# Three edits to a float32 hybrid decoder layer: single PSUM banks in the first feed-forward layer, weight sums made in place, three load buffers

## The chip, the core and the metric

The kernel runs on one core of a Trainium2 chip. Times are device microseconds of that core. The time before is 1018.22 us, the median of three runs (1017.96 to 1020.32). One more execution was profiled. It took 1021.12 us, and the span from its first to its last instruction is 1019.4 us.

Five engines work side by side, each through its own queue in order: TensorE (PE, its weight loads PEld), VectorE (DVE), ScalarE (ACT), GpSimd (POOL) and SyncE (SP), whose queue issues most DMAs. They wait for each other by semaphores.

## The reference

One decoder layer over 512 tokens and 16 learned meta tokens (528 rows), width 1024, all in float32: a half-step SwiGLU feed-forward layer, a mixer with a gated short convolution group and a forgetting-attention group, a second half-step feed-forward layer, and a last norm.

```
h = h + 0.5 * swiglu_ffn(rms_norm(h, ffn1_norm), ffn1_w_gu, ffn1_w_down)
h = h + hybrid_mixer(rms_norm(h, mix_norm), w_in, conv_w, b_f, ...) 
h = h + 0.5 * swiglu_ffn(rms_norm(h, ffn2_norm), ffn2_w_gu, ffn2_w_down)

def swiglu_ffn(h, w_gu, w_down):
    gate, up = jnp.split(h @ w_gu, 2, axis=-1)
    return (jax.nn.silu(gate) * up) @ w_down
```

`w_gu` is 1024 x 5632 and `w_down` 2816 x 1024. The change is in the two feed-forward layers.

## The kernel before

**Split operands.** Activations lie transposed (128 of the 1024 columns by tokens). Every operand is split into a high and a low part of a faster matmul type, and each product is three matmuls: high by high, high by low, low by high. ScalarE makes the high part (`hi`, line 497, a CAST into `w_hi`), VectorE the low part (`lo`, line 501, into `w_lo`). The DMA-loaded weight tile is `raw`.

**Seven products for eight.** Most of a feed-forward layer runs in *units*. A unit multiplies a 2 x 2 block of weight tiles M11, M12, M21, M22 (for `nj` pairs of row blocks) by two halves of the tokens, with seven products in place of eight, by sums of weights and sums of activations. `prep` (line 460) loads and makes the weights, `products` (line 513) writes the matmuls. A gate or an up unit has `nj` = 4, here called wide; a `down` unit has `nj` = 3, 2 or 4. A product is 3 `nj` matmuls, so a unit of `nj` = 4 has 84.

**Weight sums before.** Two tiles are loaded for a unit: `raw["all"]` (all four blocks, line 474) and `raw["ss"]` (M11 and M12 a second time, line 470). Two DMAs from POOL's queue add to `ss` in flight (`add`, line 478), M12 and M22, so that it holds M11+M12 and M12+M22. VectorE makes `s24` in a tile of its own (lines 482, 485): M12+M22+M11, and that plus M21. `hi` and `lo` are made of four sources: `nat` (M11 and M21), `ss`, `s24` and `22` (M22).

**Slots.** The order of the work is written out by `Slots`: a list of PE slots, one product each, and for every slot a list of tasks of the other engines, sorted by a priority, emitted behind the slot's matmuls. A unit that begins at slot b has seven slots:

- b: A = first product; b+1: the previous unit's last product (`p4`, into the previous B); b+2: second product into A; b+3: B (`s24`); b+4: E; b+5: B again; b+6: C; its own `p4` follows at b+8.
- ScalarE seeds B with -A (line 540, task at b+1, before slot b+3; bank A is read while slot b+2 waits to write it) and C with -B (line 541, task at b+4, before slot b+5).
- VectorE and ScalarE read A, B, C and E out between b+3 and b+9 (in `down`, line 609 and lines 612, 613 add them to `hT`).

A, B and C come in pairs used by turns, E is one bank. In the second feed-forward layer each is a tile of one bank from the pool `banks`. In the first, A, B and C are tiles `acc` of two banks each, one for each turn (`new1`, lines 624 and 735), so both turns of B, for example, are one tile.

**Around it.** `pair_forms` (line 371) makes the activation sums: four POOL operations (lines 379 to 382), then ScalarE and VectorE splits (lines 368, 369), as tasks `t1 + e` and one later. The first four hidden tiles of the first layer and the next ones (`classical`, line 407) are ordinary products. `Weights` feeds the mixer and has the first two hidden tiles; the fourth accumulator of that stage, `a3`, stays in PSUM and is multiplied there (lines 715, 746 to 749).

Of the kernel before, what the change touches and what calls it, by code (L numbers as in the profile page):

```python
# [14 lines left out]
P = 128  # L15
# [18 lines left out]
class Weights:  # L34
# [129 lines left out]
def layer(ctx, tc, x, meta, n1, gu1, dn1, nm, w_in, conv_w, b_f, g_conv, g_attn, w_out, n2, gu2, dn2, nf, out):  # L164
# [174 lines left out]
    class Ffn:  # L339
# [116 lines left out]
        def raw(self):  # L456
            return self.pool.tile([P, 2048], F32, name="raw", bufs=2).rearrange("p (k c) -> p k c", c=256)


        def prep(self, b, mat, c0, j0, nj):  # L460
# [26 lines left out]
            def src(nm_):  # L487
                if nm_ == "nat":
                    return raw["all"][:, :, 0]
                if nm_ == "22":  # L490
                    return raw["all"][:, 1::2, 1]
                return raw[nm_].rearrange("p a b c -> p (a b) c")
# [20 lines left out]
        def products(self, nj, rhs, w):  # L513
# [109 lines left out]
    with tc.tile_pool(name="ps1", bufs=3, space=PSUM) as ps1, tc.tile_pool(name="ps1s", bufs=2, space=PSUM) as ps1s:  # L623
# [5 lines left out]
        with tc.tile_pool(name="xin", bufs=1) as xin:  # L629
# [50 lines left out]
            with tc.manual_schedule(engines={mybir.EngineType.PE, mybir.EngineType.Activation, mybir.EngineType.DVE}):  # L680
# [34 lines left out]
                a3, tile_a = new1()  # L715
# [5 lines left out]
                row_rstd(sa)  # L721
            gp = ps1s.tile([P, 512], F32, name="sm")
# [7 lines left out]
        with tc.tile_pool(name="ffn1", bufs=1, reuse_waits="tile") as pool, tc.manual_schedule(engines=ENGINES):  # L730
            sl = Slots()
            (accB, tile_b), (accC, tile_c) = new1(), new1()
            bank_e = ps1s.tile([P, 512], F32, name="sm")
            ring = lambda j: 0 if j == 10 else RING + (j + 3) % 4 * 14 * 264
            F = Ffn(gu1, dn1, 264, GN1, pool, sl, [[t[:, 0], t[:, 1]] for t in (tile_a, tile_b, tile_c)] + [bank_e], 0, ring)
            W.raw_pool = pool


            def early(f, g, u):
                def gate():  # L740
                    stt(g, g, -0.5, rs, ALU.mult, ALU.mult)
# [525 lines left out]
```

## Time and profile before

| | us |
|---|---|
| median of three runs | 1018.22 |
| lowest, highest | 1017.96, 1020.32 |
| profiled execution | 1021.12 |
| its span | 1019.4 |
| mean granted PE clock | 0.987 of full |
| busy: PE, PEld | 955.9, 907.4 |
| busy: DVE, ACT, POOL | 771.8, 563.0, 350.6 |

By stretch of the span: start and first tiles to 38; classical tiles of the first layer to 93; its units to 405; mixer to 645; classical tiles of the second layer to 692; its units to 990; last norm to 1019.4. In the first layer's units (312 us) PE is busy 286.0 us, in the second's (298 us) 288.3 us, in the mixer (240 us) 238.4 us.

How to read it: PE's busy time is modelled from the starts of matmuls that overlap. A wait is clearer on PEld, the loading of weights before a matmul, as idle time with its releaser in brackets: `[0.68 <-ACT acc L540]` means that the engine stood idle for 0.68 us, until the ScalarE instruction of line 540 on tile `acc` was done.

### The profile page before, as it was taken

The numbers are of one execution on the slowest core, as the hardware profiler recorded it, in microseconds if no ns is written. First come the engines' busy times: TensorE is split into PE (matmuls) and PEld (weight loads), VectorE is DVE, ScalarE is ACT, GpSimd is POOL, SyncE is SP. The second block draws the span as 40 slices with busy tenths as digits, with TensorE's granted clock in tenths as the row PEclk, the third lists the DMA queues.
The fourth block names the chain that finished last, engine by engine and source line by source line (L and its number), as shares of the span: only waits on it lengthen the run. The fifth ranks groups of instructions, "written<-read, shape, count | busy, mean of one in ns | idle before, by whom it ended". The sixth has DMA issues, their size and how long they took to land.

```text
span 1019.4 us, 18073 instructions
## 1 busy us (share of the span) xinstructions
PE 955.9 (94%) x7022; PEld 907.4 (89%) x7022; DVE 771.8 (76%) x1252; ACT 563.0 (55%) x981; POOL 350.6 (34%) x323
## 2 busy tenths in 40 slices
PE   8899999999999987999999999999999999999995
PEld 8798999999999877989999978778998998999994
DVE  6688886787677877777767567788885887788755
ACT  5545545554556444675747555455644554566344
POOL 3356534433544462310000000265533553454302
PEclk9999999999999998999999999999998999999997
DMA  6327789869985674423322122258789979998932
GB/s 202 91 83 173 153 208 224 172 143 224 222 182 132 156 167 106 122 64 84 83 64 76 55 84 62 64 124 208 159 198 210 208 166 215 209 221 194 225 64 84
DMA packets 205414, 149.87 MB, mean 147 GB/s; under 512 B 6836, under 2 KB 204768, under 8 KB 205328
## 3 DMA queue, kind: packets, MB, share of 16 engines
q1 hardware_dynamic: 146176, 119.26, 38.6%
q0 software_dynamic: 59008, 28.93, 23.3%
q8 instruction: 55, 0.90, 0.4%
q10 hardware_dynamic: 144, 0.52, 0.1%
q14 instruction: 31, 0.25, 0.1%
HBM read 146.53 MB, written 2.10 MB: 146 GB/s over the span
## 4 chain that ended last, share of the span: by engine, by line
PE 47%; DVE 8%; issue 4%; ACT 3%; DMA 2%; POOL 1%; ACTq 0%; POOLq 0%; DVEq 0%
PE bank L527 21%; PE bank L318 17%; PE acc L527 3%; PE bank L1059 2%; DVE w_lo L501 2%; DMA ss<-in_ffn_w_down_dram 1%; DMA ss<-in_ffn_w_gu_dram 1%; PE bank L996 1%; PE bank L1026 1%; DVE arena L369 1%; ACT w_hi L497 1%; DVE w_lo L454 1%; PE sm L527 1%; PE bank L1226 1%; DVE xn L398 0%
## 5 line engine op out<-in xcount | busy, mean ns | idle before, releaser
L527 PE MATMUL bank<-arena,w_hi 128*128 128x256 f32 x1568 | 290.2, 287 | 11.8 <-ACT bank L540 5.0
L527 PE MATMUL acc<-arena,w_hi 128*128 128x264 f32 x1296 | 245.9, 289 | 26.1 <-ACT acc L540 17.6
L527 PEld LDWEIGHTS bank<-arena,w_hi 128*128 128x128 f32 x1568 | 248.2, 195 | 14.9 <-ACT bank L540 6.7
L527 PEld LDWEIGHTS acc<-arena,w_hi 128*128 128x128 f32 x1296 | 201.7, 190 | 34.5 <-ACT acc L540 24.4
L527 PE MATMUL bank<-arena,w_lo 128*128 128x256 f32 x784 | 224.1, 286 | 0.0
L318 PE MATMUL bank<-arena,w_hi 128*128 128x512 f32 (+2 forms) x896 | 203.3, 331 | 0.0
L527 PE MATMUL acc<-arena,w_lo 128*128 128x264 f32 x648 | 185.1, 286 | 0.0
L318 PEld LDWEIGHTS bank<-arena,w_hi 128*128 128x128 f32 x896 | 142.1, 188 | 15.5 <-DVE arena L973 0.2
L527 PEld LDWEIGHTS bank<-arena,w_lo 128*128 128x128 f32 x784 | 152.7, 195 | 0.0
L478 POOL DMA_DIRECT2D ss<-in_ffn_w_gu_dram x68 | 89.1, 1572 | 162.7 <-DVE w_lo L501 35.2
L501 DVE TENSOR_TENSOR w_lo<-raw,w_hi 128x1024 fp32r<-128x1024 f32 (+2 forms) x124 | 115.7, 952 | 28.3 <-ACT w_hi L497 27.7
L318 PE MATMUL bank<-arena,w_lo 128*128 128x512 f32 (+2 forms) x448 | 127.5, 331 | 3.9 <-DVE w_lo L454 3.9
L527 PEld LDWEIGHTS acc<-arena,w_lo 128*128 128x128 f32 x648 | 122.7, 189 | 0.3 <-DVE w_lo L501 0.2
L497 ACT CAST w_hi<-raw 128x1024 fp32r<-128x1024 f32 (+2 forms) x124 | 93.4, 758 | 31.3 <-PE bank L527 15.9
L478 POOL DMA_DIRECT2D ss<-in_ffn_w_down_dram x56 | 72.5, 1541 | 107.1 <-DVE w_lo L501 52.9
L497 ACT CAST w_hi<-ss 128x1024 fp32r<-128x1024 f32 (+2 forms) x62 | 59.1, 954 | 77.7 <-PE acc L527 32.5
L318 PEld LDWEIGHTS bank<-arena,w_lo 128*128 128x128 f32 x448 | 75.6, 188 | 13.6 <-DVE w_lo L454 6.0
L497 ACT CAST w_hi<-s 128x1024 fp32r<-128x1024 f32 (+2 forms) x62 | 59.2, 955 | 40.3 <-DVE s L485 34.6
L501 DVE TENSOR_TENSOR w_lo<-s,w_hi 128x1024 fp32r<-128x1024 f32 (+2 forms) x62 | 79.6, 1284 | 0.0
L81 DVE TENSOR_TENSOR w_lo<-raw,w_hi 128x1024 fp32r<-128x1024 f32 (+2 forms) x53 | 56.5, 1076 | 20.5 <-ACT w_hi L80 20.2
L501 DVE TENSOR_TENSOR w_lo<-ss,w_hi 128x1024 fp32r<-128x1024 f32 (+2 forms) x62 | 68.4, 1103 | 0.0
L80 ACT CAST w_hi<-raw 128x1024 fp32r<-128x1024 f32 (+3 forms) x54 | 44.0, 828 | 43.6 <-PE bank L318 35.4
(251 smaller groups left out, 1525.6 us busy)
## 6 DMA issues: line engine op xcount, KB each, us to landing
raw<-in_ffn_w_gu_dram SPq DMA_DIRECT2D x34, 1024.0 KB, 6.0
ss<-in_ffn_w_gu_dram SPq DMA_DIRECT2D x34, 512.0 KB, 4.9
ss<-in_ffn_w_gu_dram POOLq DMA_DIRECT2D x68, 256.0 KB, 6.1
raw<-in_ffn_w_down_dram SPq DMA_DIRECT2D x20, 768.0 KB, 4.7
raw<-in_w_in_dram SPq DMA_DIRECT2D x24, 512.0 KB, 4.1
raw<-in_ffn_w_gu_dram SPq DMA_DIRECT2D x16, 512.0 KB, 3.9
ss<-in_ffn_w_down_dram SPq DMA_DIRECT2D x20, 384.0 KB, 3.3
ss<-in_ffn_w_down_dram POOLq DMA_DIRECT2D x40, 192.0 KB, 5.7
```

The lines of the kernel that those rows point to most:

```text
L80: nc.scalar.copy(h, src)
L81: nc.vector.tensor_sub(lw, src, h.bitcast(F32))
L318: nc.tensor.matmul(ap, lhsT=wt[:, kw, :], rhs=mt[:, k, c0 - off:c1 - off], start=(first and a == 0 and b == 0), stop=(last and a == len(ks ...
L369: self.sl.at(t + 1, lambda: nc.vector.tensor_sub(lo, src(), hi.bitcast(F32)), 2)
L454: self.sl.at(t - 1, lambda: nc.vector.tensor_sub(w["w"][1], w["r"], w["w"][0].bitcast(F32)), 3)
L478: nc.gpsimd.dma_start(out=raw["ss"][:, :, i], in_=mat_j[:, i, :, c0 + P:c0 + 2 * P], accum_op=ALU.add)
L497: nc.scalar.copy(w[nm_][0][:, :m], src(nm_))
L501: nc.vector.tensor_sub(w[nm_][1][:, :m], src(nm_), w[nm_][0][:, :m].bitcast(F32))
L527: nc.tensor.matmul(bank, lhsT=wt[:, idx(j), :], rhs=r[:, form, part], start=(start and i == 0), stop=(i == last), skip_group_check=True)
L996: nc.tensor.matmul(t[:, o:o + c1 - c0], lhsT=qt[:, i * P:(i + 1) * P], rhs=kt[:, c0:c1], start=(b == 0), stop=(b == 1))
L1026: nc.tensor.transpose(o, sm[:, SOFF[i] + j * P:SOFF[i] + (j + 1) * P], ident)
L1059: nc.tensor.matmul(oo, lhsT=lt, rhs=rt, start=(a == 0 and n_ == 0), stop=(a == 1 and n_ == len(ops) - 1))
```

## The change

1. The first feed-forward layer moves out of the two-bank accumulator pool into the pool `banks`: A, B and C are now two tiles of one bank each, as in the second layer. `a3` is copied to SBUF by ScalarE first, like the other three.
2. `load_ss` and its tile go. `load` is a task at b-15 rather than b-10. ScalarE copies M11 (`base`, at b-11) into a small tile `s3`; POOL's two adding DMAs (still at b-10) put M22 onto M12 inside the loaded tile, and M12 onto `s3`. `s2` and `s4` write into the loaded tile.
3. The sources are now `nat`, `s24`, `s1` (M12+M22, and M22) and `s3` (M11+M12). `s24` stays at b, `s1` is at b+1 and `s3` at b+2, where `ss` was at b-1 and `22` at b+2.
4. `raw` has three buffers in both layers, two before.
5. The pair sums that aren't needed soon are split one slot earlier (`e` = 4).

In the changed file `base` is line 474, `s2` and `s4` lines 481 and 484, `hi` 492, `lo` 496, the matmul 522, the seeds 535 and 536.

```
-            t = self.raw_pool.tile([P, self.raw_cols], F32, name="raw", bufs=2 if self.raw_cols == 2048 else 3)
+            t = self.raw_pool.tile([P, self.raw_cols], F32, name="raw", bufs=3)
...
-            d, e = (0, 3) if soon else (1, 5)
+            d, e = (0, 3) if soon else (1, 4)
...
-            return self.pool.tile([P, 2048], F32, name="raw", bufs=2).rearrange("p (k c) -> p k c", c=256)
+            return self.pool.tile([P, 2048], F32, name="raw", bufs=3).rearrange("p (k c) -> p k c", c=256)
...
-            def load_ss():
-                raw["ss"] = self.pool.tile([P, nj, 2, P], F32, name="ss", tag="ss", bufs=2)
-                nc.sync.dma_start(out=raw["ss"].rearrange("p j i c -> p j (i c)"), in_=mat_j[:, 0, :, c])
...
+            def base():
+                raw["s3"] = self.pool.tile([P, nj, P], F32, name="s3", bufs=2)
+                nc.scalar.copy(raw["s3"], raw["all"][:, 0::2, 0])
+
             def add():
-                for i in range(2):
-                    nc.gpsimd.dma_start(out=raw["ss"][:, :, i], in_=mat_j[:, i, :, c0 + P:c0 + 2 * P], accum_op=ALU.add)
+                for i, t in ((1, raw["all"][:, 0::2, 1]), (0, raw["s3"])):
+                    nc.gpsimd.dma_start(out=t, in_=mat_j[:, i, :, c0 + P:c0 + 2 * P], accum_op=ALU.add)
 
             def s2():
-                raw["s24"] = self.pool.tile([P, 2, nj, P], F32, name="s24")
-                nc.vector.tensor_add(raw["s24"][:, 0], raw["ss"][:, :, 1], raw["all"][:, 0::2, 0])
+                nc.vector.tensor_add(raw["all"][:, 0::2, 0], raw["all"][:, 0::2, 1], raw["all"][:, 0::2, 0])
 
             def s4():
-                nc.vector.tensor_add(raw["s24"][:, 1], raw["s24"][:, 0], raw["all"][:, 1::2, 0])
+                nc.vector.tensor_add(raw["all"][:, 1::2, 0], raw["all"][:, 0::2, 0], raw["all"][:, 1::2, 0])
...
+                return raw["s3"] if nm_ == "s3" else raw["all"][:, :, 1 if nm_ == "s1" else 0]
...
-            sl.at(b - 14, load_ss, 3)
+            sl.at(b - 15, load, 3)
+            sl.at(b - 11, base, 3)
             sl.at(b - 10, add, 3)
-            sl.at(b - 10, load, 3)
             sl.at(b - 2, s2, 3)
             sl.at(b - 1, s4, 3)
-            for nm_, t in (("nat", b - 4), ("ss", b - 1), ("s24", b), ("22", b + 2)):
+            for nm_, t in (("nat", b - 4), ("s24", b), ("s1", b + 1), ("s3", b + 2)):
...
-            sl.slot(prod(B, "s24", lambda j: j, F_T2, False))
-            sl.slot(prod(E, "ss", lambda j: 2 * j + 1, F_T1, True))
-            sl.slot(prod(B, "ss", lambda j: 2 * j, F_T3, False))
-            sl.slot(prod(C, "s24", lambda j: nj + j, F_B22, False))
-            self.p4 = prod(B, "22", lambda j: j, F_T4, False)
+            sl.slot(prod(B, "s24", lambda j: 2 * j, F_T2, False))
+            sl.slot(prod(E, "s1", lambda j: 2 * j, F_T1, True))
+            sl.slot(prod(B, "s3", lambda j: j, F_T3, False))
+            sl.slot(prod(C, "s24", lambda j: 2 * j + 1, F_B22, False))
+            self.p4 = prod(B, "s1", lambda j: 2 * j + 1, F_T4, False)
...
+                t = t528("raw")
+                a3.each(lambda ps, g: nc.scalar.copy(g(t), ps))
+                raws_f.append(t)
...
-            (accB, tile_b), (accC, tile_c) = new1(), new1()
-            bank_e = ps1s.tile([P, 512], F32, name="sm")
+        bk = [[bank(), bank()] for _ in range(3)]
+        accB, accC = (Acc(b, L) for b in bk[1:])
+        bank_e = bank()
```

ScalarE's queue in the third `down` unit of the first layer's second group with `nj` = 3, before. The rows begin with the seed of B (line 540); 128x384 is the high part of `22`, the first 128x768 that of the next unit's `nat`, then follow the seed of C (line 541) and the next unit's `ss` and `s24` (`s_2734`).

```order
L540 ACTIVATE acc<-acc 128x264
L497 CAST w_hi<-raw 128x384
L497 CAST w_hi<-raw 128x768
L541 ACTIVATE acc<-acc 128x264
L497 CAST w_hi<-ss 128x768
L497 CAST w_hi<-s_2734 128x768
```

The same unit in the changed kernel; `s_2515` is this unit's `s3`, `s_2711` the `s3` of the unit two further on.

```order
L535 ACTIVATE bank<-bank 128x264
L492 CAST w_hi<-raw 128x768
L492 CAST w_hi<-s_2515 128x384
L492 CAST w_hi<-raw 128x768
L474 COPY s_2711<-raw 128x512
L536 ACTIVATE bank<-bank 128x264
L492 CAST w_hi<-raw 128x768
```

The copy of line 474 now stands in front of the seed of C (line 536). It can begin when VectorE has made the low part of `s_2515`, since `s3` has two buffers and takes turns.

VectorE's queue in the same unit, before: the low parts of `ss` and `s24`, two adds to `hT` (line 609), the low part of `22` (128x384), and that of the next unit's `nat`.

```order
L501 TENSOR_TENSOR w_lo<-ss,w_hi 128x768
L501 TENSOR_TENSOR w_lo<-s_2638,w_hi 128x768
L609 TENSOR_TENSOR hT<-acc,hT 128x264 x2
L501 TENSOR_TENSOR w_lo<-raw,w_hi 128x384
L501 TENSOR_TENSOR w_lo<-raw,w_hi 128x768
```

And in the changed kernel: the low parts of `s24`, `s1`, `s3` (`s_2515`) and the next `nat`, with the adds (now line 604) between them.

```order
L496 TENSOR_TENSOR w_lo<-raw,w_hi 128x768
L604 TENSOR_TENSOR hT<-bank,hT 128x264
L496 TENSOR_TENSOR w_lo<-raw,w_hi 128x768
L604 TENSOR_TENSOR hT<-bank,hT 128x264
L496 TENSOR_TENSOR w_lo<-s_2515,w_hi 128x384
L496 TENSOR_TENSOR w_lo<-raw,w_hi 128x768
```

The number of low parts is the same. What moved is that none is left between the sums of the weights (lines 482, 485) and the low part of `s24`, and one more stands between that and the half-size one.

## Rows read from the trace of the kernel before

**Rows 1.** PEld waits of the whole run: engine, line, releaser: total us, times, longest.

```profile
PEld acc L527 <- ACT acc L540: 24.4, 32, 2.5
PEld acc L527 <- DVE hT L609: 9.7, 6, 2.6
PEld bank L527 <- ACT bank L540: 6.7, 8, 2.2
...
PEld bank L527 <- DVE hT L609: 3.7, 2, 1.9
...
PEld bank L527 <- ACT bank L541: 2.0, 3, 0.7
```

**Rows 2.** Windows of each layer: engines' busy us (x instructions), clock, DMA share, GB/s.

```profile
150.00:200.00 50.00, 47.55 (x382) 46.48 (x381) 35.35 (x50) 27.14 (x47) 23.02 (x19) 1.00 0.90 201
900.00:950.00 50.00, 50.00 (x419) 50.00 (x418) 42.11 (x59) 30.98 (x49) 23.32 (x18) 1.00 0.92 206
```

**Rows 3.** Timeline, PEld, two units apart: start, us, instructions [idle <-releaser].

```profile
173.11 0.30 PEld L527 LDWEIGHTS acc<-arena,w_hi 128*128 128x128 f32 x2 [0.74 <-ACT acc L540]
...
195.11 0.30 PEld L527 LDWEIGHTS acc<-arena,w_hi 128*128 128x128 f32 x2 [0.74 <-ACT acc L540]
```

**Rows 4.** Timeline, ACT, the seed of B, first layer.

```profile
205.66 0.38 ACT L540 ACTIVATE acc<-acc 128x264 f32<-128x264 f32 x1 [1.63 <-PE acc L527]
```

**Rows 5.** PEld waits from 374 to 402 us.

```profile
PEld acc L527 <- DVE hT L609: 6.8, 3, 2.6
```

**Rows 6.** Timeline, DVE, last `down` group of the first layer.

```profile
385.70 2.07 DVE L501 TENSOR_TENSOR w_lo<-s,w_hi 128x768 fp32r<-128x768 f32 x1
387.69 0.76 DVE L609 TENSOR_TENSOR hT<-acc,hT 128x264 f32<-128x264 f32 x2
```

**Rows 7.** Timeline, PEld, a joint of the second layer.

```profile
768.82 0.30 PEld L527 LDWEIGHTS bank<-arena,w_hi 128*128 128x128 f32 x2 [1.93 <-DVE hT L609]
...
770.85 0.50 PEld L527 LDWEIGHTS bank<-arena,w_hi 128*128 128x128 f32 x2 [0.89 <-ACT bank L540]
```

**Rows 8.** The chain that ended last, around the joint: start, us, what.

```profile
759.38 4.92 DMA ss<-in_ffn_w_gu_dram
```

**Rows 9.** Timeline, DVE, at the joint.

```profile
767.74 0.69 DVE L482 TENSOR_TENSOR s<-ss,raw 128x512 f32<-128x512 f32 x1 [3.46 <-issue]
```

**Rows 10.** Timeline, PEld, a joint of the first layer.

```profile
364.08 0.30 PEld L527 LDWEIGHTS acc<-arena,w_hi 128*128 128x128 f32 x2 [1.62 <-DVE hT L609]
```

**Rows 11.** Timeline, ACT, end of the first stage.

```profile
30.44 2.05 ACT L712 COPY raw<-acc 128x528 f32<-128x528 f32 x3
```

**Rows 12.** Timeline, ACT, the narrow unit whose queues are shown.

```profile
233.44 0.50 ACT L497 CAST w_hi<-raw 128x384 fp32r<-128x384 f32 x1
...
236.08 0.38 ACT L541 ACTIVATE acc<-acc 128x264 f32<-128x264 f32 x1 [0.33 <-PE acc L527]
```

**Rows 13.** Timeline, ACT, a `down` unit at the end.

```profile
964.81 0.59 ACT L1168 COPY hT<-bank 128x512 f32<-128x512 f32 x1 [3.12 <-PE bank L1167]
965.30 1.05 ACT L497 CAST w_hi<-raw 128x1024 fp32r<-128x1024 f32 x1
966.24 0.38 ACT L541 ACTIVATE bank<-bank 128x256 f32<-128x256 f32 x1
```

**Rows 14.** Timeline, DVE, that narrow unit of rows 12.

```profile
235.33 1.41 DVE L501 TENSOR_TENSOR w_lo<-raw,w_hi 128x384 fp32r<-128x384 f32 x2
```

**Rows 15.** Timeline, DVE, a narrow unit behind a pair sum.

```profile
746.74 1.41 DVE L501 TENSOR_TENSOR w_lo<-raw,w_hi 128x384 fp32r<-128x384 f32 x2
```

**Rows 16.** Timeline, ACT, the same unit.

```profile
746.67 0.37 ACT L541 ACTIVATE bank<-bank 128x256 f32<-128x256 f32 x1 [0.32 <-PE bank L527]
```

**Rows 17.** Timeline, POOL, a pair sum beside a wide unit.

```profile
192.77 1.60 POOL L379 TENSOR_TENSOR ts<-s 128x264 f32<-128x264 f32 x1 [3.60 <-DVE s L582]
```

**Rows 18.** Timeline, DVE, the same stretch.

```profile
192.54 1.22 DVE L501 TENSOR_TENSOR w_lo<-ss,w_hi 128x1024 fp32r<-128x1024 f32 x1
193.68 1.77 DVE L501 TENSOR_TENSOR w_lo<-s,w_hi 128x1024 fp32r<-128x1024 f32 x1
```

More of the change, by code (lines that the diff above doesn't have):

```diff
@@ L487, in src @@
             def src(nm_):
[L488 to L492, printed above, removed]
+                return raw["s3"] if nm_ == "s3" else raw["all"][:, :, 1 if nm_ == "s1" else 0]
             def hi(nm_):
                 w[nm_] = (wts.tile([P, 8, P], F32R, name="w_hi"), wts.tile([P, 8, P], F32R, name="w_lo"))
-                m = nj if nm_ == "22" else 2 * nj
+                m = nj if nm_ == "s3" else 2 * nj
@@ L728, in layer @@
             W.done(False)
-        with tc.tile_pool(name="ffn1", bufs=1, reuse_waits="tile") as pool, tc.manual_schedule(engines=ENGINES):
-            sl = Slots()
-            (accB, tile_b), (accC, tile_c) = new1(), new1()
-            bank_e = ps1s.tile([P, 512], F32, name="sm")
[L734 to L741, printed above, removed]
-                    act(g, g, AF.Silu)
-                def up():
-                    stt(g, g, -0.25, rs, ALU.mult, ALU.mult)
-                    hd = u
-                    if isinstance(u, Acc):
-                        hd = t528("hd")
-                        u.each(lambda ps, c: nc.vector.tensor_mul(c(hd), ps, c(g)))
-                    else:
-                        nc.vector.tensor_mul(u, u, g)
-                    F.hd[f] = hd
-                return gate, up
-            for i, (f, g, u) in enumerate(((0, raws_f[0], raws_f[1]), (1, raws_f[2], a3))):
-                gate, up = early(f, g, u)
-                sl.at(2 * i, gate, 0)
-                sl.at(2 * i + 1, up, 0)
-            F.hidden_pair(0, 5, 5, True)
-            NC1 = 6
-            hx = []
-            for f in range(2, NC1):
-                t = F.classical(f, accB, accC, x1, hd_pool=pool if f < 4 else None)
-            n0 = len(sl.pe)
-            for j in range(ND // 2):
-                F.x_pair(j, 9 + 5 * j)
-            for j in range(1, NC1 // 2):
-                F.hidden_pair(j, n0 + 5 * j - 4, n0 + 5 * j - 4, True)
-            def g_units(fs):
-                for f in fs[::2]:
-                    F.gates(f)
-                    t = F.ups(f)
-                    F.hidden_pair(f // 2, t, t)
-            g_units(range(NC1, 8))
-            for m in range(0, ND, 2):
-                F.down(0, 3, m)
-            g_units(range(8, 14))
-            for m in range(0, ND, 2):
-                F.down(3, 3, m)
-            g_units(range(14, NF))
-            for m in range(0, ND, 2):
-                F.down(6, 2, m)
-            for m in range(0, ND, 2):
-                for i, t in enumerate(F.down(8, 3, m)):
-                    def fin(d=m + i):
-                        operand(d, GMIX, L, xm)
-                        squares(d, L, nc.gpsimd)
-                    sl.at(t, fin, 1)
-            n = len(sl.pe)
-            F.end()
-            W.n_used = 4
-            for i in range(2):
-                sl.at(n - 10 + 6 * i, W.load, 4)
-                sl.at(n - 5 + 5 * i, lambda: W.split(False), 4)
-            sl.run()
@@ L804, in new, with early, gate, up @@
         return Acc([bank() for _ in range(1 if n <= 512 else 2)], n)
+    with tc.tile_pool(name="ffn1", bufs=1, reuse_waits="tile") as pool, tc.manual_schedule(engines=ENGINES):
+        sl = Slots()
+        bk = [[bank(), bank()] for _ in range(3)]
+        accB, accC = (Acc(b, L) for b in bk[1:])
+        bank_e = bank()
+        ring = lambda j: 0 if j == 10 else RING + (j + 3) % 4 * 14 * 264
+        F = Ffn(gu1, dn1, 264, GN1, pool, sl, bk + [bank_e], 0, ring)
+        W.raw_pool = pool
+        def early(f, g, u):
+            def gate():
+                stt(g, g, -0.5, rs, ALU.mult, ALU.mult)
+                act(g, g, AF.Silu)
+            def up():
+                stt(g, g, -0.25, rs, ALU.mult, ALU.mult)
+                nc.vector.tensor_mul(u, u, g)
+                F.hd[f] = u
+            return gate, up
+        for i, (f, g, u) in enumerate(((0, raws_f[0], raws_f[1]), (1, raws_f[2], raws_f[3]))):
+            gate, up = early(f, g, u)
+            sl.at(2 * i, gate, 0)
+            sl.at(2 * i + 1, up, 0)
+        F.hidden_pair(0, 5, 5, True)
+        NC1 = 6
+        hx = []
+        for f in range(2, NC1):
+            t = F.classical(f, accB, accC, x1, hd_pool=pool if f < 4 else None)
+        n0 = len(sl.pe)
+        for j in range(ND // 2):
+            F.x_pair(j, 9 + 5 * j)
+        for j in range(1, NC1 // 2):
+            F.hidden_pair(j, n0 + 5 * j - 4, n0 + 5 * j - 4, True)
+        def g_units(fs):
+            for f in fs[::2]:
+                F.gates(f)
+                t = F.ups(f)
+                F.hidden_pair(f // 2, t, t)
+        g_units(range(NC1, 8))
+        for m in range(0, ND, 2):
+            F.down(0, 3, m)
+        g_units(range(8, 14))
+        for m in range(0, ND, 2):
+            F.down(3, 3, m)
+        g_units(range(14, NF))
+        for m in range(0, ND, 2):
+            F.down(6, 2, m)
+        for m in range(0, ND, 2):
+            for i, t in enumerate(F.down(8, 3, m)):
+                def fin(d=m + i):
+                    operand(d, GMIX, L, xm)
+                    squares(d, L, nc.gpsimd)
+                sl.at(t, fin, 1)
+        n = len(sl.pe)
+        F.end()
+        W.n_used = 4
+        for i in range(2):
+            sl.at(n - 10 + 6 * i, W.load, 4)
+            sl.at(n - 5 + 5 * i, lambda: W.split(False), 4)
+        sl.run()
     with ExitStack() as mix:
```

4 lines of the change are left out of this document (2 added, 2 removed).

## The prediction

> **What bounds the kernel now.** I read the stretches' busy times first: in both layers of units PE is the bound, and the other engines matter only where PE waits for them. Then the waits of PEld, which say for whom [rows 1]. The largest is for the seed of B: 32 waits, 24.4 us, one in each of the 32 units of the first layer; the second layer, with 30 units, has eight such waits, 6.7 us. The windows agree [rows 2]: in 50 us of the first layer PE is idle 2.45 us and starts 382 matmuls, in the second it is never idle and starts 419. Part of that is the width of the products (264 columns against 256). From one unit's start of B to the one two further on are 195.11 − 173.11 = 22.0 us, 11.0 for 84 matmuls, with a wait of 0.74 in each [rows 3].
>
> Why the first layer waits: the two turns of B are one tile. The seed may write it only when the last product of the unit before, which goes into the other turn, is done. That is one slot later than the seed's own source is ready. ScalarE idles 1.63 us with PE as releaser, then takes 0.38 us for the seed [rows 4], while PE has nothing to go on with.
>
> **Part 1, single banks: gains.** With a tile for each bank the seed waits only for slot b, and has slots b+1 and b+2 to run in. What the second layer shows is then the measure: its 6.7 us hold 0.89 at each of two joints (below), so 4.9 in 30 units, or 4.9 x 32/30 = 5.2 in 32. Gain 24.4 − 5.2 = 19.2 us. Ends: all 24.4, or half, 12, if the seeds come late for another reason.
>
> The same split frees slot b+3 of the last `down` group from VectorE's adds on the other turn: three waits, 6.8 us [rows 5]. These don't go away. The low part of `s24`, which the slot needs anyway, starts at 385.70 and takes 2.07, to 387.77; the two adds behind it run to 388.45, the first until about 388.1 [rows 6]. So the wait ends about 0.4 earlier, three times: 1.2 us. Ends: 0.9 and 6.8.
>
> **Parts 2 to 4, loads and sums: gains.** At the two joints of the second layer (from one set of pair sums to the next) PE waits 3.7 us in all for `hT` [rows 1], once 1.93 us and then 0.89 for the seed behind it [rows 7]. The chain shows where from: the transfer into `ss` lasts from 759.38 to 764.30 [rows 8], and VectorE, which has waited 3.46 us, can start `s2` only at 767.74 [rows 9]: its adding DMAs come late, and everything behind `s2` on VectorE's queue with them. In the changed kernel the load is issued five slots earlier, the second load of the same bytes is gone, and three buffers let it go ahead; the adds find their data there. I take all of it: 3.7 + 2 x 0.89 = 5.5, and 1.62 at the joint of the first layer [rows 10], together 7.1. Ends: 0 (the adds stay late for another reason) and 9.7 less 6.8, plus 5.5, that is 8.4.
>
> Gains in all: 19.2 + 1.2 + 7.1 = 27.5 us.
>
> **Costs.** (a) *The copy of `a3`* goes in front of the first split of the next stage: three such copies take 2.05 us [rows 11], one 0.7.
>
> (b) *`base`* is a new ScalarE instruction in each of 62 units, in front of the seed of C. No row has it. A cast of 128x384 took 0.50 [rows 12], a copy of 128x512 from PSUM 0.59 [rows 13]; I take these. It also waits for VectorE's low part of the unit's `s3`, and behind it in ScalarE's queue stands the seed, for which PE waits. In the ordinary narrow unit the half-size low part starts at 235.33; the row's 1.41 us cover it and the next one of twice its size, so it takes 0.47 and ends at 235.80 [rows 14]. Then `base` to 236.39, the seed to 236.77. Before, the seed starts at 236.08, when PE has finished B's part [rows 12]; the product E keeps PE 9 x 0.124 (47.55 us by 382) = 1.1 us, to about 237.1. Slack 0.3: no stall. Wide units have a product of 12 x 0.124 = 1.5 and some 0.7 of slack; but one seed in several meets a late low part, so I put 0.1 on each of the 30 that are not counted below: 3.0 (ends 0 and 30 x 0.59 = 18).
>
> (c) *Narrow units behind a pair sum's splits* have VectorE later against PE. There the half-size low part starts at 746.74 and ends at 747.21 [rows 15], `base` ends at 747.7 and the seed at 748.1; PE, which released the old seed at 746.67 [rows 16], needs it at 746.5 + 9 x 0.119 = 747.5. Stall 0.6, in five such units: 3.0 (ends 0 and 24 narrow units by 0.6 = 14).
>
> (d) *Second layer's last `down` group*: its seeds of C are late already, 2.0 us in three waits [rows 1], because a copy of hT at 964.81 and a cast of 1.05 stand ahead of them [rows 13]. `base` goes between: 0.6 twice, 1.2 (ends 0 and 2.4 for four units).
>
> (e) *First layer's last `down` group*: the low part of `s1` (0.94: 1.41 − 0.47) [rows 14] now stands behind the adds, where `ss` was split before them, in an idle time of VectorE. One such low part on the path in two of four units: 2.0 (ends 0 and 3.8).
>
> Removed loads (62 by up to 0.5 MB) cost PE nothing now: DMA is busy 0.90 to 0.92 of the time [rows 2], but PE waits on none except at the joints. The earlier splits (part 5) cost nothing: they only move ahead by a slot in a queue with VectorE idle 8 to 15 of 50 us.
>
> Costs: 0.7 + 3.0 + 3.0 + 1.2 + 2.0 = 9.9 us. Net 27.5 − 9.9 = 17.6. The profiled execution took 1021.1, so 1003.5; the median of the runs lies 2.9 below that execution, so 1000.6, say 1001. Moving the terms (b) to (e) and the gain at the joints by half each way gives 995 to 1007.
>
> **The rivals.** *A. The low part of `s3` is late beside POOL.* While POOL made a pair sum (1.60 us from 192.77) [rows 17], a VectorE low part that began inside it took 1.77 where the one before took 1.22 [rows 18]: 0.55 more. The Trainium skill (SBUF — State Buffer, "SBUF: two separate sides") says that a VectorE operation with two SBUF inputs and a GpSimd one that reads SBUF lock each other out for a whole instruction; by that the loss would be up to POOL's 1.60, and the trace agrees only in part, with 0.55. Now three low parts and two adds stand in a row between `s24` and `base`, so what is lost in the row reaches the seed of C. With pair sums beside 16 wide units and about 0.7 us for each (0.55 and the term above), 11.2 us are given back: 1012 (1008 to 1015). For it: VectorE is busy 42 of 50 us in the second layer [rows 2]. Against: the wide units' slack.
>
> *B. The copies cost nothing*, since VectorE, freed of the wait for the adding DMAs, runs ahead in all units: 27.5 − 0.7 = 26.8, so 991.4.
>
> *C. Slower: `base` stalls ScalarE in every unit.* If the low part of `s3` ends 1 us later against PE than where the half-size one ends now, because two sources of full size are split after `s24` rather than one before it, the seed of C misses its slot by 0.8 in 24 narrow units (1.0 less 0.3, and the longer copy) and by 0.5 in 38 wide ones: 38 us against 26.8, so 1029. It decides from a mean stall of 27/62 = 0.43 us a unit. Against it: the low parts follow the order in which PE needs them, and VectorE is idle 15 of 50 us in the first layer.
>
> *D. The change doesn't do what it says*: the seed of B stays late, because ScalarE's queue ahead of it (casts that wait for buffers of `w_hi` to come free) only now becomes the limit; what is won at the joints pays for the copies: about 1018.
>
> **How the numbers follow.** Likeliest 0.52, A 0.20, B 0.13, D 0.07, C 0.08. A measurement of this kernel can tell a difference of over 0.3%, about 3 us. Likeliest, A and B are faster: 0.85; D the same: 0.07; C slower: 0.08. The range takes in A's and B's times, 991 to 1013, and leaves out C and D.
>
> **What would show it.** Right: PEld's waits for the seed of B fall from 24.4 to about 5 us in the first layer, and a window there has some 395 matmuls (two waits of 0.7 less in 22 us); the waits for `hT` at the joints go, and so does VectorE's 3.46 ahead of `s2`; new waits of some 0.5 us for the seed of C, behind narrow units and at the end, of 5 to 10 us in all; those for `hT` in the first layer's last group stay near 6. For A, PEld waits for the seed of C in wide units beside pair sums, with VectorE's low parts above 1.5 us. For C, a wait there in every unit, with ScalarE's `base` idle ahead of it until VectorE is done. The forecast is wrong if the seeds of B still end the waits of most units, or if those of C cost over 15 us.

## The result, and the profile after

The changed kernel takes 1002.11 us (median of four runs, 1000.34 to 1003.54), the kernel before 1018.09 (four runs). The ratio is 0.9843, with a 95% interval of 0.9814 to 0.9872: 16 us faster. The forecast was 1001. The profiled execution of the changed kernel took 1000.34 us (span 998.6, mean clock 0.988), 20.8 less than the profiled one of before. It is the fastest of its kernel, and the one of before was slower than all four timed ones, so some 5 us of the 20.8 are chance.

PEld's waits of the whole run, after (engine, line, releaser: total us, times, longest); they answer to [rows 1]:

```profile
PEld bank L522 <- ACT bank L536: 14.0, 19, 1.5
...
PEld bank L522 <- ACT bank L535: 6.6, 7, 2.7
PEld bank L522 <- DVE w_lo L496: 5.9, 6, 2.0
...
PEld bank L522 <- DVE hT L604: 0.5, 1, 0.5
```

The seed of B (line 535) holds PE 6.6 us in both layers, where lines 540 took 24.4 and 6.7. The waits for `hT`, 13.4 before, are down to 0.5. Two rows are new in size: the seed of C (line 536), 14.0 where line 541 took 2.3, and low parts, 5.9 where there were 0.2. Windows of 50 us of each layer, after, as in [rows 2]:

```profile
150.00:200.00 50.00, 50.00 (x412) 50.00 (x411) 40.83 (x55) 31.16 (x54) 23.15 (x19) 1.00 0.75 158
900.00:950.00 50.00, 47.87 (x396) 47.24 (x396) 38.12 (x55) 28.22 (x45) 19.69 (x14) 1.00 0.71 153
```

In the first layer PE is now never idle in this window and starts 412 matmuls for 382. DMA is busy 0.75 for 0.90. The second window, over the last `down` group, shows the other side: 2.13 us of idle PE, in waits for the seed of C. What stands in front of that seed shows ScalarE's timeline in a narrow unit behind a pair sum (start, us, instruction, idle before and its releaser):

```profile
132.98 0.51 ACT L474 COPY s<-raw 128x384 f32<-128x384 f32 x1 [1.00 <-DVE w_lo L496]
133.40 0.37 ACT L536 ACTIVATE bank<-bank 128x264 f32<-128x264 f32 x1
```

and VectorE's, in the same place:

```profile
132.40 0.54 DVE L496 TENSOR_TENSOR w_lo<-s,w_hi 128x384 fp32r<-128x384 f32 x1
```

`base` (line 474) idles 1.00 us until VectorE has made the low part of `s3`, then takes 0.51, then the seed 0.37; the row of PEld behind it has

```profile
133.82 0.30 PEld L522 LDWEIGHTS bank<-arena,w_hi 128*128 128x128 f32 x2 [0.67 <-ACT bank L536]
```

That is the forecast's chain of terms (b) and (c), link by link. At the end of the second layer the copy stands in front of a late seed, behind a cast, as said of [rows 13]:

```profile
943.84 1.05 ACT L492 CAST w_hi<-raw 128x1024 fp32r<-128x1024 f32 x1
944.79 0.62 ACT L474 COPY s<-raw 128x512 f32<-128x512 f32 x1
945.31 0.38 ACT L536 ACTIVATE bank<-bank 128x256 f32<-128x256 f32 x1
```

And at the joint of the second layer `s2` has no wait ahead of it any more, where [rows 9] had 3.46 us:

```profile
758.21 0.69 DVE L481 TENSOR_TENSOR raw<-raw 128x512 f32<-128x512 f32 x1
```

### The profile page after: what moved, and what is told of

It reads as the page before. It is cut to its first block, busy times and chain, and to the rows that moved or that the text cites. A ratio compares the mean times of both kernels' runs of the same rounds, so it can differ in the third digit from the quotient of the medians.

```text
span 998.6 us, 17874 instructions
## 1 busy us (share of the span) xinstructions
PE 951.8 (95%) x7022; PEld 907.8 (91%) x7022; DVE 780.3 (78%) x1260; ACT 586.1 (59%) x1044; POOL 350.9 (35%) x323
## 4 chain that ended last, share of the span: by engine, by line
PE 73%; DVE 16%; ACT 5%; issue 4%; POOL 1%; DMA 1%; SPq 0%; ACTq 0%; DVEq 0%
PE bank L522 47%; PE bank L318 19%; DVE w_lo L496 4%; DVE arena L369 3%; PE bank L1055 2%; DVE hT L604 1%; DVE w_lo L454 1%; DVE w_lo L81 1%; PE bank L992 1%; PE bank L1022 1%; ACT arena L275 1%; DVE xn L398 1%; PE acc L318 1%; DVE arena L280 1%; ACT w_hi L492 1%
## 5 line engine op out<-in xcount | busy, mean ns | idle before, releaser
L522 PE MATMUL bank<-arena,w_hi 128*128 128x256 f32 (+1 forms) x3080 | 569.4, 287 | 17.5 <-ACT bank L536 10.0
L522 PEld LDWEIGHTS bank<-arena,w_hi 128*128 128x128 f32 x3080 | 481.7, 191 | 24.1 <-ACT bank L536 14.0
L522 PE MATMUL bank<-arena,w_lo 128*128 128x264 f32 (+1 forms) x1540 | 439.4, 285 | 4.5 <-DVE w_lo L496 4.5
L522 PEld LDWEIGHTS bank<-arena,w_lo 128*128 128x128 f32 x1540 | 294.8, 191 | 6.1 <-DVE w_lo L496 5.9
L318 PE MATMUL bank<-arena,w_hi 128*128 128x264 f32 (+2 forms) x1152 | 247.3, 323 | 3.1 <-ACT w_hi L450 3.1
L492 ACT CAST w_hi<-raw 128x1024 fp32r<-128x1024 f32 (+2 forms) x186 | 176.4, 948 | 125.0 <-DVE raw L484 104.2
L496 DVE TENSOR_TENSOR w_lo<-raw,w_hi 128x1024 fp32r<-128x1024 f32 (+2 forms) x186 | 222.9, 1199 | 31.9 <-ACT w_hi L492 30.2
L318 PEld LDWEIGHTS bank<-arena,w_hi 128*128 128x128 f32 x1152 | 179.6, 191 | 18.9 <-ACT w_hi L450 3.5
L318 PE MATMUL bank<-arena,w_lo 128*128 128x264 f32 (+2 forms) x576 | 155.5, 325 | 5.4 <-DVE w_lo L454 5.3
L318 PEld LDWEIGHTS bank<-arena,w_lo 128*128 128x128 f32 x576 | 96.8, 191 | 15.9 <-DVE w_lo L454 8.4
L478 POOL DMA_DIRECT2D s<-in_ffn_w_gu_dram x34 | 49.7, 1462 | 67.9 <-ACT bank L536 65.9
L81 DVE TENSOR_TENSOR w_lo<-raw,w_hi 128x1024 fp32r<-128x1024 f32 (+2 forms) x53 | 55.3, 1052 | 21.0 <-ACT w_hi L80 20.8
L604 DVE TENSOR_TENSOR hT<-bank,hT 128x264 f32<-128x264 f32 (+1 forms) x112 | 47.5, 424 | 14.5 <-PE bank L522 14.1
L474 ACT COPY s<-raw 128x512 f32<-128x512 f32 (+2 forms) x62 | 35.5, 572 | 17.6 <-DVE w_lo L496 15.2
```

What stands on the lines that cost most here:

```text
L81: nc.vector.tensor_sub(lw, src, h.bitcast(F32))
L318: nc.tensor.matmul(ap, lhsT=wt[:, kw, :], rhs=mt[:, k, c0 - off:c1 - off], start=(first and a == 0 and b == 0), stop=(last and a == len(ks ...
L474: nc.scalar.copy(raw["s3"], raw["all"][:, 0::2, 0])
L478: nc.gpsimd.dma_start(out=t, in_=mat_j[:, i, :, c0 + P:c0 + 2 * P], accum_op=ALU.add)
L522: nc.tensor.matmul(bank, lhsT=wt[:, idx(j), :], rhs=r[:, form, part], start=(start and i == 0), stop=(i == last), skip_group_check=True)
L604: return lambda: nc.vector.tensor_add(t, ps, t)
```

## The experiments

Each experiment was timed in five or six runs (e2 in twelve) beside the kernel before on the same chip. The medians of before differ between chips (1018.1 to 1021.3 us), so a difference in us between kernels of two chips can be off by some 3 us, and the ratios are the better measure.

A part of the differences is TensorE's clock, whose mean changes from run to run. The kernel before, on one chip, took 1015.45 us in a run with a mean granted clock of 0.993 and 1023.78 in one with 0.982. The last column takes (1 - clock) x span off each run, an estimate of what the lower clock cost it. With that, the medians of the kernel before are 1006.0 to 1006.4 on the three chips of the experiments.

| kernel | us | ratio to before | 95% interval | us, less clock (estimate) |
|---|---|---|---|---|
| the change | 1002.11 | 0.9843 | 0.9814 to 0.9872 | 988.8 |
| e1: edit 1 alone | 1010.29 | 0.9908 | 0.9874 to 0.9942 | 995.6 |
| e2: edits 2 to 5 alone | 1022.06 | 1.0015 | 0.9996 to 1.0034 | 1008.3 |
| e4: the change, base behind the seed | 994.38 | 0.9749 | 0.9717 to 0.9782 | 980.4 |
| e5: the change, squares added by VectorE | 996.78 | 0.9776 | 0.9746 to 0.9806 | 987.1 |
| e6: e4 and e5 | 987.80 | 0.9702 | 0.9675 to 0.9728 | 980.0 |
| e7: e5, base on VectorE | 993.97 | 0.9753 | 0.9727 to 0.9780 | 982.4 |
| e8: the change, two load buffers | 1278.80 | 1.2553 | 1.2517 to 1.2588 | 1168.9 |
| e9: the change without edit 5 | 1004.40 | 0.9851 | 0.9826 to 0.9875 | 994.8 |
| e10: e1 with thin adding DMAs | 990.25 | 0.9695 | 0.9671 to 0.9720 | 978.4 |
| e11: e6, last nat later | 989.15 | 0.9684 | 0.9659 to 0.9708 | 978.4 |
| e12: e2, base behind the seed | 1011.52 | 0.9910 | 0.9883 to 0.9936 | 996.8 |

**e1, edit 1 alone.** The kernel before, with `a3` copied and the first layer's accumulators in `banks`; nothing in `prep`.

> The kernel before with edit 1 alone (six single banks for A, B and C and one for E in the first layer, a3 copied). Theory: the shared two-bank tile is the whole of the gain on the seed of B. The 32 waits of 24.4 us fall to about 4; the waits for hT at the joints stay, since loads and sums are as before; no copy stands in front of the seed of C. 1018.1 - 20.5 - 1.2 + 0.7 = 997 us (995 to 1000), which is less than the 1002.1 of the full change. Rival: a part of the gain on the seeds comes from the earlier loads and the other order of the splits; then seeds of B still wait in many units and the time stays above 1005.

Measured: 1010.29, a miss by 13 us on the high side. PEld's waits in e1:

```profile
PEld bank L527 <- ACT bank L540: 13.1, 17, 2.2
PEld bank L527 <- DVE hT L609: 10.2, 8, 2.8
...
PEld bank L527 <- ACT bank L541: 7.1, 8, 1.8
PEld bank L527 <- DVE w_lo L501: 6.2, 5, 2.1
```

The regular wait in each unit is gone, as the theory has it. But others came up, at joints of the first layer above all (line 541 up to 1.8 us). ScalarE's timeline in e1, where the longest of them begins, shows for what:

```profile
145.66 1.04 ACT L497 CAST w_hi<-raw 128x1024 fp32r<-128x1024 f32 x1 [3.07 <-DMA raw<-in_ffn_w_gu_dram]
146.61 0.37 ACT L541 ACTIVATE bank<-bank 128x264 f32<-128x264 f32 x1
```

The cast of `nat` waits 3.07 us for the load itself, and the seed of C behind it is late. SP's queue had issued that load at 136.48:

```profile
136.48 0.37 SPq L474 DMA_DIRECT2D raw<-in_ffn_w_gu_dram  x1
```

So the 1 MB load was on its way for 9 us. Before, PE's 0.7 us in each unit had given the loads more time; e10 tests that reading.

**e2, edits 2 to 5 alone.** The changed kernel's `prep`, buffers and splits, with the two-bank tiles.

> The kernel before with edits 2 to 5 alone (sums in the loaded tile, base copied by ScalarE, three load buffers, earlier splits); the first layer keeps its two-bank tiles. Theory: the joints win 7 us, and the seeds of C that come late behind the copy cost about 11 to 12 (14.0 us of such waits after the change against 2.3 before), less what the seeds of B, which still wait 0.7 us in each unit of the first layer, give time for: 1018 to 1023 us. Rival: the in-place sums are a gain of their own; then 1012 or less.

Measured: 1022.06, within what was expected; no gain. Its PEld waits:

```profile
PEld acc L522 <- ACT acc L535: 23.7, 32, 2.7
...
PEld acc L522 <- ACT acc L536: 6.4, 8, 2.1
...
PEld bank L522 <- ACT bank L536: 5.7, 8, 1.2
```

The seed of B still waits in all 32 units, and the seeds of C cost 12.1. The two parts are not additive: 0.9908 x 1.0015 = 0.9923 against 0.9843 for both, 8 us more in the whole than in the parts.

**e10, what holds the loads in e1.**

```
-                    nc.gpsimd.dma_start(out=raw["ss"][:, :, i], in_=mat_j[:, i, :, c0 + P:c0 + 2 * P], accum_op=ALU.add)
+                    nc.gpsimd.dma_start(out=raw["ss"][:, :1, i], in_=mat_j[:, i, :1, c0 + P:c0 + 2 * P], accum_op=ALU.add)
```

> The single banks alone (1010.3 us), with the two adding DMAs of each unit cut to the first of their nj pairs of row blocks, which leaves the other sums of the weights out: a wide unit moves 1.5 + 0.125 MB in place of 2. It tells what holds the loads back once PE no longer waits for the seed of B. Theory: the transfers themselves (a 1 MB load took 8.9 us beside the others, where the slots from the release of its buffer to the cast of nat are shorter than that in a narrow unit); with less to move, the waits at the joints (hT 10.2 us, seed of C 7.1, low parts 6.2 in all) lose 8 us or more: 1000 to 1003 us. Rival: the release of the two load buffers and the order of SP's and GpSimd's queues hold the loads; the waits stay within 3 us and the time at 1008 to 1011.

Measured: 990.25, 20 us less than e1, more than the theory asked for. PEld's waits in e10:

```profile
PEld bank L527 <- ACT bank L540: 8.2, 12, 2.1
PEld bank L527 <- DVE w_lo L501: 5.8, 6, 2.1
...
PEld bank L527 <- ACT bank L541: 3.3, 5, 0.7
PEld bank L527 <- DVE hT L609: 2.3, 2, 1.5
```

Buffers, queues and orders are those of e1; the kernel leaves out the sums of all but the first pair of row blocks. The waits of the four rows fall from 36.6 to 19.6 us. ScalarE's casts of weights had waited 27.0 us for transfers in e1, and wait 1.1 in e10; the largest such row of e1, and the only one of e10:

```profile
ACT w_hi L497 <- DMA ss<-in_ffn_w_gu_dram: 12.0, 3, 4.8
```

```profile
ACT w_hi L497 <- DMA raw<-in_ffn_w_down_dram: 1.1, 1, 1.1
```

So the transfers held e1 back, and the rival, the release of two buffers, does not decide there by itself. One thing is not told apart: the thin adding DMAs also keep GpSimd busy for less (1.04 us each on the mean, for 1.56). The run also says what the single banks are worth where loads are in time: e10 is 3.0% faster than before (the gain at the second layer's joints is in it), e1 0.9%.

**e8, the third buffer.**

```
-            return self.pool.tile([P, 2048], F32, name="raw", bufs=3)...
+            return self.pool.tile([P, 2048], F32, name="raw", bufs=2)...
```

> The changed kernel with two load buffers for the weights of the feed-forward layers, as before, in place of three. Theory: the third buffer is what lets loads start early; with two, a load waits until the unit two before has made its last low part, the sums come late again, and PE waits at joints and in other units as with the single banks alone (1010.3): 1006 to 1011 us. Rival: one load less for each unit is enough, since the transfers then take less time: 1001 to 1004.

The first line of the code shown for the change goes back as well. Measured: 1278.8, 277 us slower than the change; neither theory nor rival. PEld's waits, and after them ScalarE's timeline in one unit of e8:

```profile
PEld bank L522 <- ACT bank L536: 208.6, 60, 5.0
```

```profile
194.46 0.62 ACT L474 COPY s<-raw 128x512 f32<-128x512 f32 x1 [4.01 <-DMA raw<-in_ffn_w_gu_dram]
194.98 0.37 ACT L536 ACTIVATE bank<-bank 128x264 f32<-128x264 f32 x1
```

The chain of waits in the same place (start, us, what):

```profile
188.01 1.23 DVE w_lo L496
...
189.25 5.13 DMA raw<-in_ffn_w_gu_dram
```

The low part of `s1` of an earlier unit frees the buffer at 189.24, the load goes out at once and lasts 5.13 us, `base` waits for it, and the seed of C, which needs none of it, stands behind `base`. This looks like the forecast's rival C, a stall in every unit, at 3.5 us a unit (208.6 by 60), but has the load as its cause rather than the low part of `s3`. The clock adds to it: from 93 to 400 us of e8, with PE waiting in each unit, it was granted at 0.88 on the mean; in the change's units (93 to 405) it was 0.99. Two windows of e8 show the two levels, 1.2 and 2.4 GHz. The first lies 1.2 us behind a wait of 4.2 us of PE, the second in the same stretch of matmuls (length, PE's busy time and matmuls first, the clock behind the fifth engine):

```profile
182.30:185.50 3.20, 3.20 (x16) 3.20 (x16) 1.82 (x4) 1.05 (x1) 1.04 (x1) 0.51 0.96 115
186.20:189.40 3.20, 3.20 (x28) 3.20 (x27) 1.82 (x4) 2.12 (x4) 0.00 (x0) 1.00 0.12 14
```

A third buffer is therefore a condition of edit 2, since that edit puts a load in ScalarE's path to PE.

**e4, base behind the seed.**

```
-            sl.at(b - 11, base, 3)
+            sl.at(b - 10, base, 3)
```

> The changed kernel, with the copy of M11 (base) one slot later, so that it stands behind the seed of C in ScalarE's queue and no longer in front. Theory: the copy and its wait for VectorE's low part are what makes the seeds of C late; their 19 waits of 14.0 us fall to some 6 of 4, nothing else waits, and the time falls by 8 to 10 to 992 to 994 us. Rival 1: the seeds of C are late because of the casts and other copies ahead of them; waits and time stay (1002). Rival 2: the second adding DMA, which waits for base, comes a slot later and the sums at the joints are late again: 3 to 7 us of the gain go, 996 to 1001.

Measured: 994.38, 8 us less than the change and just above what was expected. PEld's waits in e4:

```profile
PEld bank L522 <- ACT bank L535: 8.8, 10, 2.7
...
PEld bank L522 <- DVE w_lo L496: 6.4, 7, 2.0
...
PEld bank L522 <- ACT bank L536: 2.5, 4, 0.7
PEld bank L522 <- DVE hT L604: 2.5, 5, 1.5
```

The seeds of C fall from 14.0 to 2.5. Four us come back at two other rows: the next seed of B and `hT`, which are next in line. So "nothing else waits" was wrong, but the place of one copy in ScalarE's queue was worth half as much again as the change had won. Of the rivals, the second (sums late again at the joints) does not show.

**e12, the same step on e2.** The same edit, on edits 2 to 5 alone.

> Edits 2 to 5 alone on the kernel before (1022.1 us, when base stands in front of the seed of C), with base one slot later, behind the seed. Theory: what made edits 2 to 5 alone no gain is only this copy; its 16 waits for the seed of C (12.1 us) fall to 3 or 4, and the time to 1012 to 1015 us. Rival: with the seed of B still late in each unit of the first layer, PE's other waits take up the slack, and the time stays above 1018.

Measured: 1011.52, just below what was expected, 0.9910 for 1.0015. The seeds of C cost 2.0 us for 12.1:

```profile
PEld bank L522 <- ACT bank L536: 2.0, 3, 0.7
```

Edits 2 to 5 are a gain of their own, 9 us, that the place of `base` had eaten up. The parts don't add here either: 0.9908 x 0.9910 = 0.9819, against 0.9749 for e4, which has both.

**e5, squares added by VectorE.** The add of GpSimd in `squares`, in the last group of the first layer:

```
...
-                    squares(d, L, nc.gpsimd)
+                    if d == 0:
+                        squares(d, L)
+                    else:
+                        sq["t"] = t528("sq")
+                        nc.scalar.activation(sq["t"], hT[:, d], AF.Square)
+                def fin2(sq=sq):
+                    if sq:
+                        nc.vector.tensor_add(ssum[:, :L], ssum[:, :L], sq["t"])
                 sl.at(t, fin, 1)
+                sl.at(t + 1, fin2, 1)
```

> The changed kernel, with the seven adds of squares in the first layer's last group made by VectorE, one task later, in place of GpSimd. Theory: VectorE's low parts there are stretched (2.08 us where 0.94 is usual) while GpSimd adds squares (1.3 to 1.7 us) because the two engines hold each other up; without GpSimd they take 0.94 each again, PE's four waits for low parts fall from 5.2 to below 2 us, less 0.7 for an add that stands ahead of one: 999 to 1001 us. Rival: VectorE's queue is simply too long there; the stretched records are waits of another kind and stay above 1.5 us, the adds come on top, and the time is 1003 to 1006.

Measured: 996.78, lower than expected, 5 us less than the change in medians and 3.8 in the profiled executions. In the change, VectorE's timeline has

```profile
373.87 2.09 DVE L496 TENSOR_TENSOR w_lo<-raw,w_hi 128x768 fp32r<-128x768 f32 x1
...
378.11 1.66 DVE L496 TENSOR_TENSOR w_lo<-s,w_hi 128x384 fp32r<-128x384 f32 x1
```

beside GpSimd's adds:

```profile
373.83 1.30 POOL L290 TENSOR_TENSOR ssum<-ssum,sq 128x528 f32<-128x528 f32 x1 [1.62 <-ACT sq L289]
377.75 1.60 POOL L290 TENSOR_TENSOR ssum<-ssum,sq 128x528 f32<-128x528 f32 x1 [2.61 <-ACT sq L289]
```

and in e5, the same two low parts, with the adds now its own:

```profile
373.31 0.95 DVE L496 TENSOR_TENSOR w_lo<-raw,w_hi 128x768 fp32r<-128x768 f32 x1
...
374.52 0.70 DVE L799 TENSOR_TENSOR ssum<-ssum,sq 128x528 f32<-128x528 f32 x1
...
377.03 0.55 DVE L496 TENSOR_TENSOR w_lo<-s,w_hi 128x384 fp32r<-128x384 f32 x1
```

The low parts take 0.95 and 0.55 again. An add of 1.30 us on GpSimd had cost VectorE 1.14, and takes it 0.70 to do itself. PEld's waits for low parts fall from 5.9 to 3.8 us, less than was expected, since the adds stand ahead of low parts now.

The time fell by more than the waits, and that is not this edit's theory: the granted clock was 0.989 to 0.991 in all runs of e5, for 0.984 to 0.988 in the change's. With the clock taken off, 1.7 us are left of the 5. Why the clock was higher stays open; from 360 to 402 us, where the adds are, it was 1.00 in the profiled executions of both.

**e6, both.** The edits of e4 and e5 together.

> The changed kernel with both: base one slot later (behind the seed of C), and the adds of squares in the first layer's last group on VectorE. Theory: the two losses lie in different stretches and don't share a cause, so the gains add: 1002.1 - 7.7 - 5.3 = 989 us (988 to 991). Rival: what one frees, the other uses up (VectorE in the last group runs on the edge in both): 992 to 994.

Measured: 987.80, just below what the theory has; the fastest kernel of the study together with e11, 1.4% below the change. PE waits 2.5 us for seeds of C and 4.0 for low parts there. In PEld's waits for seeds, low parts and `hT` the two gains do add: 27.0 us in the change, 20.2 in e4, 25.5 in e5, 18.4 in e6. But of the 6.6 us between e4 and e6 most is the clock again; less clock, 0.4 is left.

**e7, base on VectorE.** On e5:

```
-                nc.scalar.copy(raw["s3"], raw["all"][:, 0::2, 0])
+                nc.vector.tensor_copy(raw["s3"], raw["all"][:, 0::2, 0])
```

> As the changed kernel with the adds of squares on VectorE, but base copied by VectorE in its old place, right behind the low part that frees its buffer, so that ScalarE neither copies nor waits. Theory: it is only the place in ScalarE's queue that costs; the 19 waits for the seed of C fall to 6 or fewer as with the copy behind the seed, and the time is 988 to 991 us. Rival: VectorE has no room for 62 copies of about 0.5 us (31 us more on 780); waits for low parts and for hT rise by 5 us or more in all, and the time is 993 to 998.

Measured: 993.97, in the rival's range. The waits:

```profile
PEld bank L522 <- ACT bank L535: 10.5, 12, 2.6
...
PEld bank L522 <- DVE w_lo L496: 5.4, 7, 1.4
PEld bank L522 <- DVE hT L604: 3.5, 8, 1.7
...
PEld bank L522 <- ACT bank L536: 2.5, 4, 0.7
```

The seeds of C are as early as in e6, so it was ScalarE's queue that delayed them. But the rows of VectorE and of what follows it are 3.5 us longer than in e6 (10.5, 5.4 and 3.5 for 9.5, 4.0 and 2.4), less than the rival's 5. The rest of the 6 us between the two has no row of its own, and the clock can account for it: 0.988 in the profiled execution of e7, 0.993 in that of e6. Less clock, 2.4 us are left of the 6.

**e9, without edit 5.**

```
-            d, e = (0, 3) if soon else (1, 4)
+            d, e = (0, 3) if soon else (1, 5)
```

> The changed kernel without edit 5 (the splits of pair sums that aren't needed soon stay five slots behind). Prediction's step: this edit costs and brings nothing, 1002.1 within 1.5 us. Rival: one slot later the split leaves VectorE free for the low part of s3 in the narrow units behind a pair sum, and two or three of the waits for the seed of C go: 999 to 1000; or later splits make a product wait for its activations: over 1004.

Measured: 1004.40; its interval and that of the change overlap, so the time alone decides nothing (less clock, e9 is 6 us slower). The trace does show a loss: waits for low parts are 10.0 us in eleven, for 5.9 in six. One of the five new ones, on PEld, and what VectorE does ahead of that low part:

```profile
133.15 0.19 PEld L522 LDWEIGHTS bank<-arena,w_lo 128*128 128x128 f32 x1 [0.67 <-DVE w_lo L496]
```

```profile
130.97 1.26 DVE L369 TENSOR_TENSOR arena<-ts,arena 128x1056 fp32r<-128x1056 f32 x1
```

Four of the five lie in narrow units behind pair sums, where the late split (line 369) stands ahead of the low part of `s24`. The forecast's step that edit 5 costs nothing holds, but it also brings something: it keeps some 4 us of waits away. In e1, without edits 2 to 5, no narrow unit behind a pair sum has such a wait.

**e11, the last nat later.** On e6, in the second layer's last group, the high part of `nat` at b-3 and its low part at b-2.

> The best so far (987.8 us: base behind the seed of C, squares added by VectorE), and in the second layer's last down group the high and low part of nat one slot later, so that the cast of 1.05 us stands behind the seed of C too. Theory: the three waits of 0.67 for the seed of C there go, nothing takes their place: -2 us, 986 (985 to 988). Rival: the product A of the next unit waits for its low part, and the time stays.

Measured: 989.15, not to be told apart from e6. Of the three waits for the seed of C there one is left, and one of 0.45 for a seed of B is new; some 1 us at most.

## Why the prediction was right

The time, the sign and, in the main, the mechanism came out. By its own steps, in us of PEld's waits, from the profiled executions before and after:

| step | forecast | measured |
|---|---|---|
| seed of B, first layer | -19.2 | 24.4 to 3.8: -20.6 |
| joints | -7.1 | -7.1; two more hT waits -0.8 |
| other seeds of B, second layer | 0 | -2.1 |
| first layer's last group, slot b+3 | -1.2 | hT 6.8 to low parts of `s24` 4.2: -2.6 |
| copy of a3 | +0.7 | next matmul at 40.99, was 40.02: +1.0 |
| (b) wide units | +3.0 | one wait, +0.7 |
| (c) narrow units behind pair sums | +3.0 | eight waits, +4.7 |
| units with nj = 2 | none | four waits, +3.15 |
| (d) second layer's last group | +1.2 | 2.0 to 3.4: +1.4 |
| (e) first layer's last group | +2.0 | low part of `s1`: none; of `s3` +1.5; seeds of C 0.3 to 2.0: +1.7 |
| sum | -17.6 | -19.0 |

That the sums are so close is in part luck. The gains came out 5.7 us larger than forecast and the costs 4.3 larger, and most of that cancels. Of its signs, that of 5 to 10 us for the seeds of C was passed: 14.0 is near the 15 that it had named as a sign of being wrong. That of some 395 matmuls in the window was too low by its own rows: 382, with 0.74 of every 11 us idle, make some 410 without that wait.

**Edit 1.** Right: the seed's wait went with the shared tile, and the 3.8 us left (2.7 of them in the first unit) are near the 5.2 that the second layer had suggested. Rival D has no ground: ScalarE's queue ahead of the seed had room.

**Joints.** The gain is as large as forecast. What the step left unsaid is its other half. It called the second load free for PE, with DMA busy 0.90 of the time and no wait except at the joints, and added the terms as if each stood alone. e1 and e10 show that they do not: with PE faster by 0.7 us a unit, the old loads take back about 10 of the 20 us, and edits 2 to 4 are what keeps them. The sum for both was right since both were made; the same sum for edit 1 alone was wrong by 13.

**`base`.** Right in kind, and mis-sized in place: 7.2 us forecast for (b) to (d), 10.0 measured. Wide units have slack enough, all but one. In narrow ones behind pair sums eight seeds were late, not five. The smallest units were counted with the narrow ones: with nj = 2 the product E, which has to cover copy and seed, has 6 matmuls, about 0.75 us by the 0.124 of [rows 2], where that of nj = 3 has 1.1. e4 shows that most of this was a matter of place. Term (e) came to 3.2 for 2.0, and by another way: no wait in that group was for a low part of `s1`.

**Rival A** had its place wrong. PE has no wait for a seed of C beside the pair sums of wide units, but for one, in the first layer's second unit; the low part ahead of it is of 128x512, that of a wide unit:

```profile
114.20 0.68 DVE L496 TENSOR_TENSOR w_lo<-s,w_hi 128x512 fp32r<-128x512 f32 x1
...
115.76 0.30 PEld L522 LDWEIGHTS bank<-arena,w_hi 128*128 128x128 f32 x2 [0.73 <-ACT bank L536]
```

The stretch itself is real, and larger than [rows 18] made it: in the last group a low part of 0.94 took 2.09 beside an add of 1.30 on GpSimd, so it lost 1.14 of 1.30; and e5 shows that it goes when GpSimd is silent. Beside [rows 18] alone the lock for a whole instruction that the Trainium skill states (SBUF — State Buffer, "SBUF: two separate sides") had looked too strong; these rows agree with it, and so does [rows 18] if it is read again: the low part of 1.77 began 0.91 us after GpSimd's sum of 1.60, so that at most 0.69 was left to lose, and 0.55 was lost. The same stretch is what [rows 6] showed without being read: the 2.07 us on which the step about slot b+3 rests were a stretched 0.94, and the step took them as given. GpSimd, before, in the place of rows 6:

```profile
385.67 1.28 POOL L290 TENSOR_TENSOR ssum<-ssum,sq 128x528 f32<-128x528 f32 x1 [3.46 <-ACT sq L289]
```

**Rival B** (991) is near the kernel with the copies out of the way: e4 reached 994. **Rival C** did not come; a stall in every unit came only with two buffers, and from the load (e8).

What stays open: about 2 us by which the profiled spans differ beyond the waits (the clock, 0.987 and 0.988, is a part of them); and why the clock is higher in the runs of some kernels (e5, e6, e9) than of others (e4).

## What to carry to other kernels

When a regular stall of the bounding engine is removed, ask in the same breath what had lived from it: here the loads had used PE's 0.7 us a unit, and without lighter loads half of the gain went back to them. A helper instruction is priced by what it waits for and by what stands behind it in its engine's queue: one copy of 0.5 us, one place further on, was worth 8 us. A row that takes twice its usual time beside another engine's work is a finding, not a price. And where two kernels differ by 5 us in 1000, the granted clock of their runs comes first: it was most of what e5 and e6 seemed to win over the change and over e4.

## What the runs showed of the hardware

- VectorE's low parts (two SBUF sources) took 2.09 and 1.66 us beside GpSimd's adds of 1.30 and 1.60, and 0.95 and 0.55 without them. The work cost less on VectorE itself (0.70) than the wait for it.
- The queue of the adding DMAs is dear for its bytes. Queues of the page before (packets, MB, share of 16 engines):

```profile
q1 hardware_dynamic: 146176, 119.26, 38.6%
q0 software_dynamic: 59008, 28.93, 23.3%
```

  In share by MB that is 0.32% against 0.81%, 2.5 times as much for the queue that holds the adding ones. Its packets are smaller (490 bytes on the mean for 816), and by packet it is 1.5 times as much, so the price of adding and that of small packets are not told apart. In e10 the second row falls to 8.22 MB and 6.9%.
- In e8, with waits of 3.5 us in each unit, the granted clock was 0.88 on the mean from 93 to 400 us, though PE was busy 234 of these 307 us. At the lower level PE started 16 matmuls in 3.2 us, at the upper 28.
